# Projection phase of a hybrid mLSTM and attention layer: separate PSUM banks for units and operand products, and another order in the last block

## Chip, cores, metric

One core of a Trainium2 chip. The metric is the device time of one execution in microseconds (us); lower is better. The kernel runs one decoder layer over 2048 tokens of width 1024.

## What is computed

The layer is a sandwich-normalised token mixer and an MLP. The mixer has one combined input projection; its columns feed a 4-head mLSTM (a chunked linear recurrence with a causal convolution on q and k, a state C, and output gates) and an 8-head latent attention, whose q, k and v come by a second product from normalised low-rank latents. Cut to what matters:

```python
def token_mixer(a, cos, sin, w_in, ..., w_out):
    proj = a @ w_in
...
    qk_ml = jax.nn.silu(causal_conv(qk_ml, conv_w, conv_b))
...
    h_ml = mlstm_chunkwise(q_ml, k_ml, v_ml, gates[..., :ML_HEADS], gates[..., ML_HEADS:])
    h_ml = rmsnorm(h_ml, ml_head_norm)
    h_ml = h_ml * jax.nn.sigmoid(o_ml)
    q = rmsnorm(c_q, q_norm) @ w_uq            # rotary on 32 of 96 columns a head
    kv = rmsnorm(c_kv, kv_norm) @ w_ukv        # 64 of k and 64 of v a head
...
    h_mla = causal_block_attention(q, k, v)
    return jnp.concatenate([h_ml, h_mla], axis=-1) @ w_out
```

Then `x + rmsnorm(mix)`, and `x + rmsnorm(relu(m @ w_up) ** 2 @ w_down)`.

## The kernel before

Every fp32 product is three matmuls on values split into a high and a low part (mm3, L244 to L247): high by high, low by high, high by low. A "step" below is one such group of three.

The program is written by a small list scheduler, the class Plan (L125). Each operation names its engine, a planned duration, a key (smaller is more urgent), the operations it comes after, the rings it takes a buffer from and the operations that give a buffer back. Plan runs this once on the host and so fixes one static order for each engine; on the chip each engine goes through its own list in order, and waits where a semaphore is not there yet. An operation that waits therefore holds all that stands behind it on its engine.

**Projection.** The tokens go in four blocks of 512 (NB). In a block PE works on units of eight steps each: 13, 14, 15 the latents, 0 the gates and rotary keys of the recurrence, 1 to 4 the convolved q and k, 5 to 8 the values (here called mv_0 to mv_3, one for 128 tokens each), 9 to 12 the output gates (mm_9 to mm_12). From the latents come operand products: kp_0 to kp_3 and vp_0 to vp_3 of one step each, qp_0 to qp_3 and rp_0, rp_1 (the rotary part of q) of two steps each. MIXED and LASTLINE (L98, L323) list gates and products in the wished order, and from the list each gets its time, which is its key. In blocks 0 to 2 the values come ahead of MIXED; in block 3 LASTLINE has them last.

**PSUM.** Units and products share one ring, "mm", of two banks (psm, L306 and L310). A unit is read by one instruction: DVE for a gate (L1177), ACT for values (L1150). A k, v or q product is read by two: ACT copies the high part (L766, for v L817), DVE copies the raw value (L769, for v L820); both come after the product and are planned at 570 and 690 ns, and the ring's buffer is free when both are done. Pool then makes the low part (L772), and SP stores it (L796, L831, L844). An r product has three DVE readers (L876, L880, L883).

**Chunks.** chunk (L1181) does the recurrence for 128 tokens: scores S, a transpose kt, the numerator num (four matmuls on vext and the state C), the state products kv_c_0 and kv_c_1 (they need kw, which DVE makes from kt, L1243), then on DVE, ACT and Pool the normalised state hn (L1282), its transpose ht on PE (L1289), and ho = ht times the gate (L1293). hn has two buffers (HN), so hn of chunk 2 can only be written once ht of chunk 0 has been read.

**Into attention.** When the last unit is done, switch2 (L1436) gives the projection's space to attention. The row maxima of head 0 and query block 0 (m_0_0_0 and so on, L1578, reduced on DVE, L1583 and L1585; their transposes mt) come ahead of the scores S (L245 with QK). The QK operands are loaded on SP's queue: rotary keys krd (L1526), qkd (L1532), qrd (L1534), the mask (L1471).

## Time and profile before

| | |
|---|---|
| median of 3 runs | 2426.09 us (2425.77 to 2426.1) |
| profiled execution, span | 2425.1 us |
| mean granted clock of TensorE | 0.994 |
| busy: PE, DVE, ACT, POOL | 2375.4, 1750.1, 1363.0, 833.1 us |
| projection with the way into attention | about 0 to 550 us |

A row of the timeline shows start, duration, engine, line, operation, output<-inputs, and in brackets the idle time before it with what ended it. A row of the table by stretches shows for each engine busy time and number of instructions, then the clock granted to TensorE (PEclk, 1.00 is full), the DMA engines' share and GB/s. A matmul's row runs to the modelled end of its pipeline, so rows that follow each other overlap.

### The profile page before, as it was taken

The numbers are of one execution on the slowest core, as the hardware profiler recorded it, in microseconds if no ns is written. First come the engines' busy times: TensorE is split into PE (matmuls) and PEld (weight loads), VectorE is DVE, ScalarE is ACT, GpSimd is POOL, SyncE is SP. The second block draws the span as 40 slices with busy tenths as digits, with TensorE's granted clock in tenths as the row PEclk, the third lists the DMA queues.
The fourth block names the chain that finished last, engine by engine and source line by source line (L and its number), as shares of the span: only waits on it lengthen the run. The fifth ranks groups of instructions, "written<-read, shape, count | busy, mean of one in ns | idle before, by whom it ended". The sixth has DMA issues, their size and how long they took to land.

```text
span 2425.1 us, 33998 instructions
## 1 busy us (share of the span) xinstructions
PE 2375.4 (98%) x10943; PEld 1918.9 (79%) x10943; DVE 1750.1 (72%) x3149; ACT 1363.0 (56%) x2646; POOL 833.1 (34%) x717
## 2 busy tenths in 40 slices
PE   9899999999999999999999999999999999999996
PEld 7777787777777777788788888888888888888885
DVE  6966565658888887746866687766675677676778
ACT  5635454437778778544666566755664343443454
POOL 2635334437888888522000000000000322322346
PEclk9999999999999999999999999999999999999999
DMA  7686979789222321567877697666674545445458
GB/s 280 204 315 219 346 241 327 260 217 200 60 54 56 81 59 22 155 187 240 270 225 215 205 311 235 204 170 178 178 216 142 161 126 182 129 137 173 127 136 166
DMA packets 341307, 449.20 MB, mean 185 GB/s; under 512 B 34908, under 2 KB 227432, under 8 KB 341128
## 3 DMA queue, kind: packets, MB, share of 16 engines
q1 hardware_dynamic: 337192, 440.16, 59.4%
q0 software_dynamic: 3936, 6.87, 2.0%
q8 instruction: 86, 1.41, 0.2%
q14 instruction: 93, 0.76, 0.1%
HBM read 295.97 MB, written 153.05 MB: 185 GB/s over the span
## 4 chain that ended last, share of the span: by engine, by line
PE 54%; DVE 1%; DMA 0%; issue 0%; ACT 0%; DVEq 0%; POOL 0%; POOLq 0%; ACTq 0%
PE op L245 1%; PE op L247 1%; PE op L246 1%; PE d_0X L2519 1%; PE d_4X L2519 1%; PE d_0X L2520 1%; PE d_4X L2521 1%; PE d_2X L2519 1%; PE d_1X L2519 1%; PE d_1X L2520 1%; PE d_2X L2521 1%; PE d_3X L2519 1%; PE d_3X L2521 1%; PE d_1X L2521 1%; PE d_4X L2520 1%; PE d_3X L2520 1%
## 5 line engine op out<-in xcount | busy, mean ns | idle before, releaser
L2557 POOL TENSOR_TENSOR y<-vd_0X,y 128x512 f32<-128x512 f32 x7 | 10.6, 1514 | 725.4 <-ACT vd_0X L2554 725.4
L1642 ACT ACTIVATE ph<-S 128x512 fp32r<-128x512 f32 (+1 forms) x320 | 170.4, 533 | 87.2 <-PE S L247 53.3
L1677 POOL TENSOR_TENSOR t<-t,ph 128x512 f32<-128x512 f32 (+1 forms) x192 | 212.9, 1109 | 18.1 <-ACT ph L1642 7.7
L2469 ACT CAST hh<-hr 128x512 fp32r<-128x512 f32 (+1 forms) x208 | 116.4, 567 | 158.0 <-DMA hr<-hd 20.5
L1650 DVE TENSOR_TENSOR pl<-S,ph 128x512 fp32r<-128x512 f32 (+3 forms) x272 | 157.2, 589 | 30.5 <-ACT S L1646 27.7
L245 PE MATMUL mm<-xh,wh 128*128 128x512 f32 x384 | 159.1, 414 | 5.4 <-DVE ks L769 2.1
L2474 DVE TENSOR_TENSOR hl<-hr,hh 128x512 fp32r<-128x512 f32 (+1 forms) x208 | 133.3, 648 | 32.5 <-ACT hh L2469 26.3
L246 PE MATMUL mm<-xl,wh 128*128 128x512 f32 x384 | 150.9, 393 | 0.7 <-DVE xl L420 0.6
L247 PE MATMUL mm<-xh,wl 128*128 128x512 f32 x384 | 150.6, 392 | 0.5 <-DVE wl L495 0.5
L1583 DVE TENSOR_REDUCE mp<-m 128x1 f32<-128x512 f32 x192 | 128.6, 681 | 18.9 <-PE m L1578 18.1
L1646 ACT ACTIVATE S<-S 128x512 f32<-128x512 f32 (+3 forms) x272 | 140.8, 518 | 0.4
L245 PE MATMUL S<-QK 97*128 97x512 f32 (+1 forms) x320 | 120.8, 377 | 2.0 <-DVE pl L1650 1.9
L1663 PE MATMUL o<-ph,V 128*128 128x512 f32 (+1 forms) x320 | 118.8, 378 | 2.5 <-DVE ot L1736 2.1
L246 PE MATMUL S<-QK 97*128 97x512 f32 (+1 forms) x320 | 117.8, 368 | 0.0
L247 PE MATMUL S<-QK 97*128 97x512 f32 (+1 forms) x320 | 117.5, 367 | 0.0
L1578 PE MATMUL m<-QK 96*128 96x512 f32 (+3 forms) x320 | 116.5, 395 | 0.7 <-DVE mp L1585 0.5
L1666 PE MATMUL o<-pl,V 128*65 128x512 f32 (+1 forms) x320 | 115.6, 362 | 0.5 <-POOL pl L1650 0.5
L245 PE MATMUL op<-wo,hh 128*128 128x512 f32 x256 | 101.2, 395 | 1.7 <-DVE osm L1967 0.9
L247 PE MATMUL op<-wo,hl 128*128 128x512 f32 x256 | 99.9, 390 | 0.0
L246 PE MATMUL op<-wo,hh 128*128 128x512 f32 x256 | 99.8, 390 | 0.0
L2308 ACT ACTIVATE t<-t 128x512 f32<-128x512 f32 x96 | 60.6, 632 | 69.5 <-DVE t L2303 68.9
L245 PEld LDWEIGHTS mm<-xh,wh 128*128 128x128 f32 x384 | 72.4, 189 | 26.2 <-DVE ks L769 2.9
(6449 smaller groups left out, 7567.0 us busy)
## 6 DMA issues: line engine op xcount, KB each, us to landing
hr<-hd SPq DMA_DIRECT2D x100, 448.0 KB
wr<-in_wu_dram SPq DMA_DIRECT2D x71, 512.0 KB
hd<-t SPq DMA_DIRECT2D x128, 256.0 KB
hd<-ts SPq DMA_DIRECT2D x96, 256.0 KB
wl<-wparts SPq DMA_DIRECT2D x45, 512.0 KB
QK<-qkd SPq DMA_DIRECT2D x32, 512.0 KB
xt<-in_x_dram SPq DMA_DIRECT2D x28, 512.0 KB
xf<-xd SPq DMA_DIRECT2D x40, 256.0 KB
```

Of the source, the lines that this page charges most:

```text
L245: pe.matmul(o, ah, bh, start=start, stop=False)
L246: pe.matmul(o, ah, bl, start=False, stop=False)
L247: pe.matmul(o, al, bh, start=False, stop=stop)
L1578: pe.matmul(ps[:, :n], Qh[s][0:96, q0 : q0 + P], Kh[s][0:96, kb * TB : kb * TB + n], start=True, stop=True)
L1583: vec.tensor_reduce(mp["t"][:, j, kb : kb + 1], ps, axis=AX.X, op=ALU.max)
L1642: act.activation(t["h"][:, :w], t["S"][:, :w], AF.Exp)
L1646: act.activation(t["p"][:, :w], t["S"][:, :w], AF.Exp)
L1650: (pool if by_pool else vec).tensor_tensor(t["l"][:, :w], t["p"][:, :w], f32(t["h"][:, :w]), ALU.subtract)
L1663: pe.matmul(o0, v[:, 0:128], t["h"][:, :w], start=start, stop=stop)
L1677: pool.tensor_tensor(to, to, hv, ALU.add)
L2474: vec.tensor_tensor(t["l", m][:, :w], t["r", m][:, :w], f32(t["h", m][:, :w]), ALU.subtract)
L2519: pe.matmul(ps, a, w[:, 0], start=start, stop=False, skip_group_check=True)
```

## The change

1. **Banks.** The ring "mm" of two becomes "mma" and "mmb" of one each. Gate units (and in block 3 the value units, together the "fillers"), and of the other units the odd ones, are in mma; all operand products and the other units are in mmb. Unit 12 of block 3 is in mmb.
2. **Keys.** A filler's steps after the first get a key later by FILL = 14, and fillers of a block are chained by gate_end. So products come between a gate's steps, not behind it.
3. **Orders.** MIXED has unit 9 ahead of the k products. LASTLINE has the values first, with q and r products between them, then 16 (the weights of k and v), gates 9 to 12 with k and v products.
4. **Space in block 3.** The weights of 12, 17 and 18 go to buffers of qbd and kT, the staged v products to the ring of raw weights, and hn and ho share their buffers chunk by chunk.
5. **Into attention.** EARLY names (0, 0): the maxima of head 0, query block 0 take a bank and a key of their own ahead of the others. The mask's load has a later key, switch2 waits for the stores of v of block 3, and the load of V for query block 1 for the last chunk's ho.

In blocks 0 to 2 PE's order becomes products between gate steps: for block 0 (a count is of matmuls) before `kp_2 x3, kp_3 x3, kt_2, ptx, kv_2_0, vp_0 x3, mm_10 x12`, after `mm_10 x6, kt_2, mm_10 x6, kv_2_0, ptx, mm_10 x3, kp_3 x3`; and before `qp_0 x6, qp_1 x6, mm_12 x24, qp_2 x6, qp_3 x6, rp_0 x6, rp_1 x3`, after `qp_0 x6, mm_12 x6, qp_1 x6, mm_12 x6, qp_2 x6, mm_12 x6, qp_3 x6, mm_12 x6, rp_0 x6`. The line numbers of the changed kernel differ: L246 to L248 are its mm3, L1330 its ht.

PE in block 1, around the transposes of the normalised state (ht_1, ht_2), before:

```order
L1289 MATMUL ht_0_2662<-cst,hn_0_2257 128x128 x4
L1289 MATMUL ht_1_2669<-cst,hn_1_2364 128x128 x4
L245 MATMUL rp_1_2655<-ch_1996,wh_18_2506 128x512
L246 MATMUL rp_1_2655<-cl_1997,wh_18_2506 128x512
L247 MATMUL rp_1_2655<-ch_1996,wl_18_2530 128x512
L1289 MATMUL ht_2_2693<-cst,hn_2_2687 128x128 x4
L1232 MATMUL num_3_2698<-vext,E_3_2297 128x129 x2
```

and after (mm_13 is the first latent unit of block 2):

```order
L1330 MATMUL ht_1_2695<-cst,hn_1_2380 128x128 x4
L246 MATMUL mm_13_2676<-xh_2_2616,wh_13_2575 128x512
L247 MATMUL mm_13_2676<-xl_2_2626,wh_13_2575 128x512
L248 MATMUL mm_13_2676<-xh_2_2616,wl_13_2573 128x512
L246 MATMUL mm_13_2676<-xh_3_2624,wh_13_2575 128x512
L247 MATMUL mm_13_2676<-xl_3_2635,wh_13_2575 128x512
L248 MATMUL mm_13_2676<-xh_3_2624,wl_13_2573 128x512
L246 MATMUL mm_13_2676<-xh_4_2641,wh_13_2575 128x512
L247 MATMUL mm_13_2676<-xl_4_2670,wh_13_2575 128x512
L248 MATMUL mm_13_2676<-xh_4_2641,wl_13_2573 128x512
L1330 MATMUL ht_2_2722<-cst,hn_2_2714 128x128 x4
```

The rotary product's last step has left the place between ht_1 and ht_2, and nine matmuls of the next block's first unit stand there. In block 0 there are twelve: three of mm_13, six of rp_1, three of mm_13.

PE in block 3, at the k products, before (mm_9 is a gate, ch and cl the latent's two parts):

```order
L247 MATMUL mm_9_4356<-xh_7_3858,wl_9_4242 128x512
L245 MATMUL kp_1_4426<-ch_4369,wh_16_4182 128x512
L246 MATMUL kp_1_4426<-cl_4370,wh_16_4182 128x512
L247 MATMUL kp_1_4426<-ch_4369,wl_16_4180 128x512
L245 MATMUL kp_2_4430<-ch_4369,wh_16_4182 128x512
L246 MATMUL kp_2_4430<-cl_4370,wh_16_4182 128x512
L247 MATMUL kp_2_4430<-ch_4369,wl_16_4180 128x512
L245 MATMUL kp_3_4446<-ch_4369,wh_16_4182 128x512
```

and after (kv_2_1 and kt_3 belong to the recurrence's chunks 2 and 3):

```order
L248 MATMUL kp_0_4760<-ch_4375,wl_16_4689 128x512
L246 MATMUL mm_9_4774<-xh_0_3582,wh_9_4717 128x512
L247 MATMUL mm_9_4774<-xl_0_3625,wh_9_4717 128x512
L248 MATMUL mm_9_4774<-xh_0_3582,wl_9_4710 128x512
L1291 MATMUL kv_2_1_4784<-vext,kw_2_4715 128x258
L246 MATMUL mm_9_4774<-xh_1_3601,wh_9_4717 128x512
L247 MATMUL mm_9_4774<-xl_1_3653,wh_9_4717 128x512
L248 MATMUL mm_9_4774<-xh_1_3601,wl_9_4710 128x512
L246 MATMUL kp_1_4792<-ch_4375,wh_16_4702 128x512
L247 MATMUL kp_1_4792<-cl_4376,wh_16_4702 128x512
L248 MATMUL kp_1_4792<-ch_4375,wl_16_4689 128x512
L1280 MATMUL kt_3_4800<-cst,kT_117 128x128 x2
```

The k products stood in a row behind a gate unit that was done; now three or six matmuls of gate 9 stand between two of them. The whole of block 3 on PE, before: `mm_9 x15, kp_0, mm_9 x9, kp_1, kp_2, kp_3, vp_0, mm_10 x24, vp_1, vp_2, vp_3, mm_11 x24, qp_0, qp_1, mm_12 x24, qp_2, qp_3, rp_0, rp_1`, then the four value units with the chunks between them, m_0_0_0 right behind the last value unit and kt_3. After: `mv_0 x24, qp_0, mv_1 x6, qp_1, mv_1 x6, qp_2, mv_1 x12, qp_3, mv_2 x9, rp_0`, the chunks' work with rp_1 and the rest of the values, `num_2, kp_0, mm_9 x3, kv_2_1, mm_9 x3, kp_1, kt_3, mm_9 x6, kp_2, kv_3_0, mm_9 x3, num_3, kp_3, mm_9 x3, kv_3_1, mm_9 x6, vp_0, mm_10 x6, vp_1, mm_10 x18, vp_2, mm_11 x6, vp_3, mm_11 x18, mm_12 x15, m_0_0_0, mm_12 x6, m_0_1_0, mm_12 x3, m_0_2_0, m_0_3_0, ht_0, ht_1, mt_0`.

SP's queue at the first loads of QK, before (L1205 and L1197 belong to the chunks):

```order
L844 DMA qkd<-qs_3_4677 64x2x512
L901 DMA qrd<-rs_3_4700 256x1x512
L901 DMA qrd<-rs_3_4715 256x1x512
L1197 DMA E_2_4833<-wd_4301 128x512
L1471 DMA maskneg<-in_consts_dram 128x512
L1526 DMA QK_4792<-krd 32x2x512 x4
L1532 DMA QK_4792<-qkd 64x4x512
L1205 DMA iwbc_2_4839<-wd_4301 64x2x128 x2
L1534 DMA QK_4792<-qrd 16x2x512 x2
```

and after (L863 stores v of block 3, L1571, L1577 and L1579 load QK):

```order
L863 DMA vd<-vs_3_4886 128x1024
L863 DMA vd<-vs_3_4910 128x1024
L863 DMA vd<-vs_3_4936 128x1024
L1571 DMA QK_4964<-krd 32x2x512
L1577 DMA QK_4964<-qkd 64x4x512
L1579 DMA QK_4964<-qrd 16x2x512 x2
L1516 DMA maskneg<-in_consts_dram 128x512
L1571 DMA QK_4964<-krd 32x2x512 x3
L863 DMA vd<-vs_3_4970 128x1024
L1577 DMA QK_4964<-qkd 64x4x512
```

The loads stood behind the rotary stores and ahead of chunk 2; now they stand behind the stores of three v products, and one more store stands among them.

The diff, cut to its core:

```diff
-EARLY = ()
+EARLY = ((0, 0),)
...
-LASTLINE = [16, "k0", "k1", 9, "k2", "k3", "v0", 10, "v1", "v2", "v3", 11, 17, "q0", "q1", 12, "q2", "q3", 18, "r0", "r1", 5, 6, 7, 8]
+LASTLINE = [5, 17, "q0", "q1", 6, "q2", "q3", 18, 7, "r0", "r1", 8, 16, 9, "k0", "k1", 10, "k2", "k3", 11, "v0", "v1", 12, "v2", "v3"]
+FILL = 14.0
...
-    psm = pp(s_x, "psm", 2, "right")
+    psm = pp(s_x, "psm", 1, "right")
...
-    MIXED = [16, "k0", "k1", 9, "k2", "k3", "v0", 10, "v1", "v2", "v3", 11, 17, "q0", "q1", 12, "q2", "q3", 18, "r0", "r1"]
+    MIXED = [16, 9, "k0", "k1", "k2", "k3", "v0", 10, "v1", "v2", "v3", 11, 17, "q0", "q1", 12, "q2", "q3", 18, "r0", "r1"]
...
+        aside = b == NB - 1 and u in (12, 17, 18)
...
+        def aside_of(i):
+            if "a" not in t:
+                t["a"] = b1.tile([P, 2, n], F32R, tag=f"kT{(b + 1) % 2}" if u == 18 else f"qbd{(b + 1) % 2}", name=f"wa{b}_{u}")
+            return t["a"][:, i]
...
-        at = TIME[b][u]
+        at = TIME[b][5] if b == NB - 1 and 5 <= u <= 8 else TIME[b][u]
...
+        gl = pl.op("X", 0, place_l, [g, *o_turn], kA(b, at - LLEAD), take=() if aside else ("wl",))
...
+        if aside:
+            o_aside[u] = (c, gl)
...
+    def filler(b, u):
+        return u in GATES or b == NB - 1 and 5 <= u <= 8
+    def place_of(b, u):
+        return "mma" if filler(b, u) and (b, u) != (NB - 1, 12) or u in (13, 15, 1, 3, 5, 7) else "mmb"
...
+        t = {"at": place_of(b, u)}
+        fill = filler(b, u)
+        behind = [gate_end[b]] if b in gate_end and fill else []
...
+                "PE", PIN, lambda k=k: mm(k), [w["op"][k], *o_x[b, k]] + ([last] if k else behind), kA(b, TIME[b][u] + (FILL if k and fill else 0.0)),
+                take=() if k else (t["at"],), free=w["free"] + x_holders[b, k],
...
+        if fill:
+            gate_end[b] = last
...
-                    q["p"] = psm.tile([P, TB], F32, tag="mm", name=f"{nm}{b}_{n}")
+                    q["p"] = psm.tile([P, TB], F32, tag="mmb", name=f"{nm}{b}_{n}")
...
-            h = pl.op("Activation", 570, hi, [g, last], key - EV, free=[("mm", first)])
+            h = pl.op("Activation", 570, hi, [g, last], key - EV, free=[("mmb", first)])
...
-            d = pl.op("DVE", 690, raw, [g, last], key - EV, free=[("mm", first)])
+            d = pl.op("DVE", 690, raw, [g, last], key - EV, free=[("mmb", first)])
...
+                ring = "awr" if b == NB - 1 else "sg"
...
+                if ring == "awr":
+                    pl.group = "in"
...
+            fill = filler(b, 5 + c)
+            behind = [gate_end[b]] if b in gate_end and fill else []
...
+                    "PE", PIN, lambda k=k: mm(k), [ws[k // 2]["op"][0], *o_x[b, k]] + ([last] if k else behind), kA(b, TIME[b][5 + c] + (FILL if k and fill else 0.0)),
+                    take=() if k else (place_of(b, 5 + c),), free=ws[k // 2]["free"] + x_holders[b, k],
...
+        hn_, ho_ = ("hn", "ho") if b < NB - 1 else ("hn", "hn") if c < 2 else ("ho", "ho")
...
-    o_s2 = pl.op("Z", 0, switch2, unit_ops + [o_s1], -KEYA)
+    o_s2 = pl.op("Z", 0, switch2, unit_ops + [o_s1, *(o_vd[4 * NB - 4 + n] for n in range(4))], -KEYA)
...
-    o_mask = pl.op("SP", 500, lambda: dma(maskneg, consts[:, K_MASK : K_MASK + 512]), [o_s1], key=EKEY - 30, kb=256)
+    o_mask = pl.op("SP", 500, lambda: dma(maskneg, consts[:, K_MASK : K_MASK + 512]), [o_s1], key=EKEY - 29, kb=256)
...
-            after = [o_s2, o_const["v0"], *([o_sc[start_of[0, qb - 2]]] if qb > 1 else o_last if qb else [])]
+            after = [o_s2, o_const["v0"], *([o_sc[start_of[0, qb - 2]]] if qb > 1 else o_chunk[NB - 1, 3]["gate"] if qb else [])]
```

More of the change, by code (lines that the diff above doesn't have):

```diff
@@ L674, in one @@
             if b == 0:
-                o = pl.op("Activation", 560, evac, [u["op"], *t.get("o", [])], key, take=take, free=[("mm", u["head"])])
+                o = pl.op("Activation", 560, evac, [u["op"], *t.get("o", [])], key, take=take, free=[(u["at"], u["head"])])
                 head = o
@@ L678, in one @@
             else:
-                o = pl.op("DVE", 660, evac, [u["op"], o_rsbc[b], *t.get("o", [])], key, take=take, free=[("mm", u["head"]), ("rsbc", o_rsbc[b])])
+                o = pl.op("DVE", 660, evac, [u["op"], o_rsbc[b], *t.get("o", [])], key, take=take, free=[(u["at"], u["head"]), ("rsbc", o_rsbc[b])])
                 head = o
@@ L1062, in g13 @@
             vec.tensor_copy(t["tm"], t["p"][:, 0:48].rearrange("p (a c h) -> p a c h", a=3, c=4))
-        G = pl.op("DVE", 660, evac, [u["op"], o_rsbc[b]], key, take=("G",), free=[("mm", u["head"]), ("rsbc", o_rsbc[b])])
+        G = pl.op("DVE", 660, evac, [u["op"], o_rsbc[b]], key, take=("G",), free=[(u["at"], u["head"]), ("rsbc", o_rsbc[b])])
         rotate(b, t, G)
@@ L1320, in chunk @@
         o = pl.op("Pool", 1000, norm4, [o, o_fill], key)
-        hn = pl.op("DVE", 800, norm5, [o], key, take=("hn",), free=[("num", n)])
+        hn = pl.op("DVE", 800, norm5, [o], key, take=(hn_,), free=[("num", n)])
         gs = [o_gate[b, i] for i in range(4)]
-        h = pl.op("PE", 440, turn_h, [hn, *gs], key, take=("aS",), free=[("hn", hn)])
-        g = pl.op("DVE", 660, gated, [h], key, take=("ho",), free=[("aS", h)])
+        h = pl.op("PE", 440, turn_h, [hn, *gs], key, take=("aS",), free=[(hn_, hn)])
+        g = pl.op("DVE", 660, gated, [h], key, take=(ho_,), free=[("aS", h)])
         out["gate"] = [g]
-        out["end"] = pl.op("SP", 500, store, [g], key, free=[("ho", g)], kb=256)
+        out["end"] = pl.op("SP", 500, store, [g], key, free=[(ho_, g)], kb=256)
     def rope_tables():
@@ L1411, in trunk @@
             chunk(b, c)
+        if b == NB - 2:
+            for u in (17, 18):
+                for o in o_aside[u]:
+                    pl.ops[o][3].extend(x for c in range(4) for x in o_chunk[b, c]["qk"])
     V = {}
```

72 lines of the change are left out of this document (39 added, 33 removed).

## The prediction

> **What bounds the kernel now.** I read the page's head first, then the busy time of each engine by stretches of 25 us, then PE's waits up to 660 us, then the timeline at the waits that looked removable. The profiled execution has a span of 2425.1 us; the median of the runs is 2426.09, so about 1.0 us lies outside the span, and I carry that over unchanged.
>
> ```profile
> span 2425.1 us, 33998 instructions
> PE 2375.4 (98%) x10943; PEld 1918.9 (79%) x10943; DVE 1750.1 (72%) x3149; ACT 1363.0 (56%) x2646; POOL 833.1 (34%) x717
> ```
>
> PE is the bound, and the most that any re-ordering can win is what PE does not fill, plus what it runs at a lower clock. The stretches say where that is.
>
> ```profile
> core 0: us, PE busy (x) PEld busy (x) DVE busy (x) ACT busy (x) POOL busy (x), PEclk, DMA share, GB/s
> 75.00:100.00 25.00, 21.95 (x106) 17.76 (x105) 24.45 (x38) 16.23 (x30) 18.13 (x15) 1.00 0.51 150
> 100.00:125.00 25.00, 21.98 (x99) 16.89 (x98) 20.66 (x39) 15.16 (x36) 20.44 (x17) 1.00 0.85 283
> 125.00:150.00 25.00, 23.71 (x111) 18.45 (x110) 22.39 (x38) 14.16 (x26) 13.04 (x9) 1.00 0.87 300
> 225.00:250.00 25.00, 23.44 (x111) 18.35 (x110) 17.03 (x38) 14.41 (x41) 16.85 (x16) 1.00 0.90 305
> 350.00:375.00 25.00, 23.78 (x111) 18.33 (x110) 17.01 (x39) 14.63 (x42) 16.38 (x17) 1.00 0.92 312
> 450.00:475.00 25.00, 21.34 (x82) 15.37 (x81) 19.24 (x23) 13.72 (x26) 18.34 (x14) 0.93 0.80 260
> 525.00:550.00 25.00, 21.73 (x89) 16.17 (x88) 18.60 (x54) 7.78 (x23) 4.80 (x9) 0.73 1.07 237
> ```
>
> The holes are the products and gates of blocks 0 to 3 (75 to 150, 225 to 250, 350 to 375, 450 to 475) and the ramp into attention (525 to 550). In the last two the granted clock falls too: 0.07 of 25 us is 1.75 us lost in the first, 0.27 of 25 is 6.75 us in the second.
>
> ```profile
> PE ht L1289 <- DVE hn L1282: 2.9, 3, 1.2
> PE mt L1609 <- DVE mp L1583: 1.9, 1, 1.9
> PE kv L1250 <- DVE kw L1243: 1.0, 1, 1.0
> ```
>
> Those three rows (us in total, times, longest) are waits that the new order touches; the rest are waits for a PSUM bank, small and many.
>
> **How long a bank is away.** Block 3 shows it, start, duration, and in brackets the idle time before:
>
> ```profile
> 453.57 0.39 PE L246 MATMUL mm<-xl,wh 128*128 128x512 f32 x1
> 453.80 0.39 PE L247 MATMUL mm<-xh,wl 128*128 128x512 f32 x1
> 454.97 0.50 PE L245 MATMUL kp<-ch,wh 128*128 128x512 f32 x1 [0.78 <-DVE gate L1177]
> 455.31 0.39 PE L246 MATMUL kp<-cl,wh 128*128 128x512 f32 x1
> ...
> 458.41 0.50 PE L245 MATMUL kp<-ch,wh 128*128 128x512 f32 x1 [1.77 <-DVE ks L769]
> ...
> 458.98 0.40 PE L247 MATMUL kp<-ch,wl 128*128 128x512 f32 x1
> 459.48 0.69 DVE L769 COPY ks<-kp 128x512 f32<-128x512 f32 x1 [0.53 <-PE kp L247]
> 460.20 0.58 ACT L766 CAST ks<-kp 128x512 fp32r<-128x512 f32 x1 [2.63 <-DVE ks L769]
> 460.84 0.79 PE L245 MATMUL mm<-xh,wh 128*128 128x512 f32 x1 [0.32 <-ACT ks L766]
> ...
> 468.44 0.50 PE L245 MATMUL vp<-wh,ch 128*128 128x512 f32 x1 [0.23 <-DVE gate L1177]
> ...
> 469.66 0.50 PE L245 MATMUL vp<-wh,ch 128*128 128x512 f32 x1 [0.26 <-DVE vs L820]
> ...
> 470.92 0.50 PE L245 MATMUL mm<-xh,wh 128*128 128x512 f32 x1 [0.29 <-DVE vs L820]
> ```
>
> Matmuls start 0.23 us apart (453.57, 453.80), so a step of three takes 0.69. A gate's bank has one reader: from the start of its last matmul to the next use 1.17 us (453.80 to 454.97). An operand product's bank has two, and ACT begins only when DVE is done: 458.98 to 460.84 is 1.86 us. The scheduler's costs let the two run side by side (both wait for the product alone) and so leave two steps of fill, 7 x 0.23 = 1.61, where 1.86 is needed: 0.25 short at each such place. The first matmul after a wait takes 0.34 to the next instead of 0.23, so each wait costs 0.11 more; and a row lasts 0.39 while the next could start after 0.23, so each listed wait hides 0.16. I add 0.27 to a listed wait.
>
> The Trainium skill, "PSUM — Partial Sum Buffer", section "PSUM bank collisions raise a hardware error", says that two engines may not touch one bank's partitions at the same time, ACT against DVE included; the trace agrees, DVE's read and then ACT's, 1.86 us. By the scheduler's costs (reads side by side) the fill would cover it; by the rows it does not.
>
> **Block 3** is re-ordered: values first, q and r products inside them, gates with k and v products last. Removed are the six waits above: 0.78 + 1.77 + 0.32 + 0.23 + 0.26 + 0.29 = 3.65, plus 6 x 0.27 = 1.62, plus the 1.75 us of low clock there: 7.0. New places, by the two bank times against the matmuls that the new order puts between: qp_1 and qp_2 (six matmuls between) 0.26 each, kp_1 and kp_2 (six and a state instruction) 0.13, gates 10 and 11 behind one product (1.17 - 4 x 0.23) 0.25 each, each with 0.11: 1.94. And a product is now early against its input:
>
> ```profile
> 448.04 0.69 DVE L1097 TENSOR_TENSOR raw<-mm,rsbc 128x512 f32<-128x512 f32 x1 [0.43 <-PE mm L247]
> ...
> 452.24 2.95 POOL L725 TENSOR_TENSOR cl<-cca,ch 128x512 fp32r<-128x512 f32 x2
> ```
>
> The q products need both of these latents. They follow one value unit, 24 matmuls or 5.5 us behind the unit that DVE reads at 448.04, so at about 453.3; the second step wants the second latent, done at 455.2 if Pool keeps its place. I take 1.0 us, bounds 0 (Pool's order moves up) and 1.2. For ACT, which casts four more weights in that stretch, 0.35 as an estimate, between 0 and one cast of the kind above, 0.58. Block 3: 7.0 - 1.94 - 1.0 - 0.35 = **3.7 us gained**, bounds 2.5 to 5.
>
> **Blocks 0 to 2: normalised state and kw.**
>
> ```profile
> 138.35 1.03 PE L1289 MATMUL ht<-cst,hn 128*128 128x128 f32 x8
> 140.73 0.75 DVE L1282 TENSOR_TENSOR hn<-num,sm 128x256 f32<-128x256 f32 x2
> 141.29 0.68 PE L1289 MATMUL ht<-cst,hn 128*128 128x128 f32 x4 [1.20 <-DVE hn L1282]
> ...
> 269.90 0.68 PE L1289 MATMUL ht<-cst,hn 128*128 128x128 f32 x4 [1.11 <-DVE hn L1282]
> ...
> 527.33 0.77 PE L1289 MATMUL ht<-cst,hn 128*128 128x128 f32 x4 [0.55 <-DVE hn L1282]
> ...
> 103.88 0.42 DVE L1243 SCALAR_TENSOR_TENSOR kw<-kt,tm 128x256 f32<-128x256 f32 x1
> 104.36 0.70 PE L1250 MATMUL kv<-vext,kw 128*128 128x258 f32 x2 [1.01 <-DVE kw L1243]
> ```
>
> ht_2 waits for hn_2, which has a buffer only when ht_0 is done. Before, three matmuls (0.69 us) stand between; now twelve in block 0 (2.76) and nine in block 1 (2.07), and block 2, which has nine in the old order, has no wait on hn (the three of the waits view are these three rows, in blocks 0, 1 and 3). 1.20 + 1.11, and 0.17 hidden in each, make **2.65 us gained**; bounds 0 (the fill hides it only if DVE is not behind) and 2.65. In block 0 kv_2_0 came straight behind kt_2 and ptx; now six gate matmuls (1.38) stand between, and the wait of 1.01, 1.1 with its restart, is gone: **1.1 gained**, bounds 0.4 to 1.2.
>
> **Blocks 0 to 2: the bank waits themselves.** Going through both orders with 1.17 and 1.86, and 0.11 for each wait, I get 3.9, 3.95 and 3.3 us before and 3.5, 4.3 and 3.45 after: pairs of products no longer stand side by side, but every product now waits for the only operand bank, and q products with six gate matmuls between are 0.25 short (four a block). **0.1 lost.** These sums leave out that DVE may be late. With two banks in turn such lateness was half covered, with one it is not: the twelve q and r places of these blocks have no spare time. An instruction of 0.69 that is met half-way costs 0.35, and DVE is busy 0.68 (17.03 of 25) to 0.83 (20.66 of 25) of these stretches: about 0.25 each, 3.0 in all, of which I take half, since the order plans for some: **1.5 lost**, bounds 0 and the rival below.
>
> **The ramp.** The last gate units now end PE's projection work, and the first four maxima (h 0, q block 0) stand inside unit 12 instead of in the last chunk.
>
> ```profile
> 526.12 0.66 PE L1578 MATMUL m<-QK 96*128 96x128 f32 x3
> 539.35 0.63 PE L245 MATMUL S<-QK 97*128 97x512 f32 x1
> 548.09 0.43 PE L245 MATMUL S<-QK 97*128 97x512 f32 x1
> 504.38 2.59 SPq L1526 DMA_DIRECT2D QK<-krd x4
> ...
> DMA to landing us min/median/max: 2.1/4.2/4.6
> ```
>
> From the first maximum to the second head's scores 22 us pass, with DVE busy 18.6 of 25: it reduces the maxima, and it still must. What chunk 3 asked of DVE there is earlier now, but the last gate's chain and the bunched ho steps come in. The gain lies between 0 and 8.6 (the wait of mt, 1.85, and the 6.75 of clock); I take the value nearest to mt's wait, **1.5 gained**. Against it: the loads of QK stood on SP at 504.38, 21.7 us ahead of the first maximum. Now they stand behind the store of vs_2, whose product is 43 matmuls (9.9 us) ahead of that maximum. Evacuation 1.86, Pool's subtraction about 1.5, the store and four loads about 2.9 (0.65 each, from 2.59 for four) and 2.1 to 4.2 to land make 8.4 to 10.5, so the margin is +1.5 to -0.6. **0.3 lost**; behind a waiting maximum stand the rest of unit 12 and everything else on PE.
>
> **Sum:** -3.7 - 2.65 - 1.1 + 0.1 + 1.5 - 1.5 + 0.3 = -7.05. 2426.1 - 7.05 = 2419.05, so **2419 us**. Its own range, from the bounds, is 2414 to 2424. After the ramp nothing in the order of attention is changed that I price.
>
> **Rivals.**
> 1. *The only operand bank makes DVE's lateness visible everywhere (slower).* Place: the 56 products of the four blocks. Price: 0.69 / 2 x 0.83 = 0.29 each, 16.2 us; with the 1.5 taken out of the sum that is -8.55 + 16.2 = +7.65, 2433.7. It beats the gains from 0.15 us a product on. For it: 24.45 of 25 DVE at 75 to 100, and the 1.77 at 458.41, a product that waited for a DVE queue. Against it: the order is planned with DVE's queue in it. Chance 0.17.
> 2. *The loads of QK come late.* If SP or the stores are 5 us behind, PE stands at the first maximum and the gain shrinks to -7.05 + 5 = about -2, 2424. For it the margin above; against it the DMA engines' share of 0.80 at 450 to 475, which leaves room. Chance 0.15.
> 3. *The clock falls in the product stretches.* Short idle times now come at every product. Row: at 100 to 125 PE is idle 3 us and the clock stays 1.00; at 450 to 475 with a 1.77 us wait it falls, at a price of 1.75. One such fall in each of blocks 0 to 2 costs 5.25: -1.8, 2424.3. The Trainium skill, "TensorE: Matmul & The Clock Gate", section "A second HAM failure mode: psum-queue depth-cycling", speaks against this change: cycling through banks makes PE idle for moments between groups, and the clock goes down and up. The trace bears that out only in block 3. Chance 0.08.
> 4. *The ramp gives all of its 8.6:* -14.15, 2412. Chance 0.10.
>
> **How the numbers follow.** The forecast has 0.50. About 0.2%, 4.85 us, is what a measurement of this kernel can tell from no change. Faster by more: 0.44 of the forecast and 0.10 of rival 4, 0.54. Within: 0.06 of the forecast, 0.12 of rival 2, 0.06 of rival 3, 0.24. Slower: rival 1 with 0.17, and 0.05 of rivals 2 and 3 where their price is doubled, 0.22. Range: from rival 4's 2412 to 2429, which is rival 1 at 0.21 us a product; beyond lie half of rival 1 and the ends of the others.
>
> **What would show it.** Right: no wait of ht on hn in blocks 0 and 1, none of kv on kw above 0.3, no clock below 1.00 between 440 and 500, and waits at q products near 0.1 listed (0.26 less the hidden 0.16). Wrong: listed waits above 0.3 at most products (rival 1), a wait of m on a DMA (rival 2), PEclk under 1.00 in the three earlier stretches (rival 3), an S of the second head over 10 us earlier than 548 (rival 4). If attention itself, after 600, changes by more than 1 us, I have missed something that is not in this list.

## The result, and the profile after

| | before | changed |
|---|---|---|
| median of 10 runs each | 2425.84 us (2422.55 to 2429.15) | 2432.43 us (2430.65 to 2435.64) |
| ratio, 95% interval | | 1.0029 (1.002 to 1.0038) |
| profiled execution, span | 2425.1 us | 2432.3 us |

The change makes the kernel slower by about 6.6 us; forecast were 2419 us, 7 us faster, with 2412 to 2429 as the range. Single runs of one kernel differ by several us, so small terms below are read in the profiles, and differences between kernels by their ratio to the kernel before, run beside them on the same chip.

From the head of the page of the changed kernel:

```profile
PE 2380.7 (98%) x10943; PEld 1917.2 (79%) x10943; DVE 1752.5 (72%) x3149; ACT 1362.2 (56%) x2646; POOL 828.7 (34%) x717
```

The work is the same. Where PE waits and where its clock falls has moved. By stretches of 25 us, the changed kernel:

```profile
core 0: us, PE busy (x) PEld busy (x) DVE busy (x) ACT busy (x) POOL busy (x), PEclk, DMA share, GB/s
75.00:100.00 25.00, 23.53 (x111) 18.57 (x110) 24.31 (x36) 15.38 (x30) 18.63 (x16) 1.00 0.46 131
100.00:125.00 25.00, 23.78 (x105) 17.51 (x103) 21.43 (x43) 16.72 (x39) 21.97 (x19) 1.00 0.87 283
125.00:150.00 25.00, 24.05 (x109) 18.18 (x108) 21.21 (x34) 13.25 (x25) 11.01 (x8) 1.00 0.95 338
225.00:250.00 25.00, 22.27 (x106) 17.62 (x106) 18.89 (x40) 16.59 (x44) 18.41 (x17) 1.00 0.88 313
350.00:375.00 25.00, 24.16 (x117) 19.33 (x116) 17.01 (x42) 15.13 (x40) 17.61 (x18) 1.00 0.91 310
450.00:475.00 25.00, 23.83 (x101) 17.96 (x100) 18.96 (x21) 11.77 (x23) 14.81 (x12) 1.00 0.68 216
525.00:550.00 25.00, 19.72 (x79) 13.00 (x78) 16.87 (x45) 5.30 (x13) 3.18 (x8) 0.80 1.07 262
550.00:575.00 25.00, 20.06 (x106) 15.55 (x104) 16.62 (x35) 14.27 (x30) 14.26 (x13) 0.96 0.97 208
```

Block 0 (75 to 150) and block 3 (450 to 475) are fuller, and the clock of block 3 is whole. Block 1 (225 to 250) is emptier. The last row is where the loss lies: PE is idle for 4.94 us in a stretch of attention that the prediction did not price. PE's waits in the changed kernel up to 660 us (total, times, longest) give it a name:

```profile
PE o L1708 <- DVE ot L1781: 5.1, 2, 4.8
PE mm L246 <- DVE gate L1217: 2.7, 3, 1.4
PE mv L247 <- DMA wl<-wparts: 2.2, 2, 1.3
PE m L1623 <- DVE mp L1630: 2.1, 2, 1.1
PE m L1623 <- DMA QK<-qrd: 1.7, 1, 1.7
...
PE qp L247 <- POOL cl L749: 0.8, 1, 0.8
```

Two of these waits in the kernel before, for the same buffers:

```profile
PE o L1663 <- DVE ot L1736: 0.9, 2, 0.6
...
PE m L1578 <- DVE mp L1585: 0.5, 1, 0.5
```

The first line is the largest of the changed kernel, and was 0.9 before. "ot" is the buffer in which an attention output is put together for its store to hT; there is one. So I followed what held it. Here is the changed kernel's timeline around that wait, ACT, DVE and PE:

```profile
573.40 0.58 ACT L1778 COPY ot<-o 64x512 f32<-64x512 f32 x1 [5.16 <-DMA hT<-ot]
574.02 0.68 DVE L1781 TENSOR_TENSOR ot<-ot,o 64x512 f32<-64x512 f32 x1 [5.05 <-ACT ot L1778]
574.84 0.76 PE L1708 MATMUL o<-ph,V 128*128 128x512 f32 x1 [4.85 <-DVE ot L1781]
...
575.90 0.63 PE L1708 MATMUL o<-ph,V 128*128 128x512 f32 x1
...
580.40 0.40 PE L1708 MATMUL o<-ph,V 128*128 128x512 f32 x1
```

Read from the bottom of the chain: PE's bank o is released by DVE, DVE waits for ACT's copy, ACT for the store of the output before it. After the wait PE's matmuls take 0.63 to 0.76 us until about 579.5, and 0.40 then: a second price, in clock. The Trainium skill, "TensorE: Matmul & The Clock Gate", section "What's actually happening", says that PE falls to half rate after an idle window of about 3.4 us and needs as long a busy one to rise; the trace agrees here, with 4.85 us of idle time and some 4.7 us of slow matmuls. It does not agree at 458.41 of the kernel before, in the prediction's rows, where the matmuls are slow after a wait of 1.77 us with 0.78 us some microseconds ahead of it.

That store stands on SP's queue. SP in the changed kernel, from the first load of QK on:

```profile
519.13 0.63 SPq L1571 DMA_DIRECT2D QK<-krd  x1
...
531.13 2.75 SPq L1579 DMA_DIRECT2D QK<-qrd  x2
533.98 3.16 SPq L1592 DMA_DIRECT2D V<-vd  x4
537.24 5.00 SPq L1338 DMA_DIRECT2D hT<-ho  x4
542.29 2.86 SPq L1592 DMA_DIRECT2D V<-vd  x4
...
566.60 0.54 SPq L1791 DMA_DIRECT2D hT<-ot  x1
```

The same queue in the kernel before:

```profile
524.79 8.84 SPq L1547 DMA_DIRECT2D V<-vd  x8
533.73 4.28 SPq L1297 DMA_DIRECT2D hT<-ho  x2
...
557.65 0.49 SPq L1746 DMA_DIRECT2D hT<-ot  x1
```

QK's loads begin 14.8 us later (504.38 before, in the prediction's rows), V's 9.2 us later, and the first output's store 8.95 us later. The eight loads of V stood together; now four, then the four stores of ho, then four. The last unit, whose space V takes, also ends later: its last matmul starts at 530.62, against 524.90 before.

What is late at the first output is its place on SP. Pool's last instruction on it ends at 559.53 in the changed kernel, and its store is issued at 566.60, 7.1 us later; before, the two stand at 557.63 and 557.65. Below I call this gap the store's wait on SP.

In numbers, from the first matmul of unit 0 to the next such mark in the two profiles: start-up +1.2 us (unit 0 begins between 26.1 and 27.5 us in the profiles of fifteen kernels here, with no order by edit, so I take this for scatter), blocks 0 to 2 +1.3, block 3 to the first score S of head 0 +0.2, from there to the first score of head 1 +5.7 (60.8 before, 66.5 after), the rest -1.3; together, within rounding, the 7.2 us between the spans.

### The profile page after: what moved, and what is told of

Its sections match the earlier page's. It is cut to its first block, busy times and chain, and to the rows that moved or that the text cites. A ratio compares the mean times of both kernels' runs of the same rounds, so it can differ in the third digit from the quotient of the medians.

```text
span 2432.3 us, 33983 instructions
## 1 busy us (share of the span) xinstructions
PE 2380.7 (98%) x10943; PEld 1917.2 (79%) x10943; DVE 1752.5 (72%) x3149; ACT 1362.2 (56%) x2646; POOL 828.7 (34%) x717
## 4 chain that ended last, share of the span: by engine, by line
PE 53%; DVE 1%; issue 0%; DMA 0%; ACT 0%; POOL 0%; DVEq 0%; SPq 0%; POOLq 0%; ACTq 0%
PE op L246 1%; PE op L248 1%; PE op L247 1%; PE d_4X L2564 1%; PE d_3X L2566 1%; PE d_2X L2566 1%; PE d_1X L2566 1%; PE d_4X L2565 1%; PE d_4X L2566 1%; PE d_3X L2565 1%; PE d_2X L2565 1%; PE d_1X L2565 1%; PE d_1X L2564 1%; PE d_3X L2564 1%; PE d_2X L2564 1%; PE d_6X L2564 1%
## 5 line engine op out<-in xcount | busy, mean ns | idle before, releaser
L246 PE MATMUL mm<-xh,wh 128*128 128x512 f32 x376 | 155.5, 414 | 4.0 <-DVE gate L1217 2.7
L248 PE MATMUL mm<-xh,wl 128*128 128x512 f32 x376 | 147.5, 392 | 1.1 <-DVE wl L506 1.1
L246 PE MATMUL S<-QK 97*128 97x512 f32 (+1 forms) x320 | 120.7, 377 | 2.2 <-DVE pl L1695 1.9
L248 PE MATMUL S<-QK 97*128 97x512 f32 (+1 forms) x320 | 116.9, 365 | 0.0
L246 PE MATMUL op<-wo,hh 128*128 128x512 f32 x256 | 101.0, 394 | 1.2 <-DVE osm L2012 0.7
L248 PE MATMUL op<-wo,hl 128*128 128x512 f32 x256 | 99.8, 390 | 0.0
L246 PEld LDWEIGHTS mm<-xh,wh 128*128 128x128 f32 x376 | 70.6, 188 | 22.6 <-DVE gate L1217 5.3
```

What stands on the lines that cost most here:

```text
L246: pe.matmul(o, ah, bh, start=start, stop=False)
L248: pe.matmul(o, al, bh, start=False, stop=stop)
```

## Theories and experiments

**R, the ramp:** the way into attention (early maxima, QK's loads behind the v products) costs the time. **B, the banks:** one operand bank costs it, all through the four blocks. After the first four runs R was narrowed to what stands on SP's queue: V's loads, the new condition on them, the first output's store. The expectations call its forms S (the space that QK and V take), V (V's loads as a whole) and C (the condition on V alone). A difference in us is that of the medians on the same chip, 5 to 11 runs of each changed kernel; the ratio is the comparison's own, which parts from the quotient of the medians by up to 0.0005, 1.2 us (in before_v_late).

Each edit goes through the scheduler, which lays the lists of PE and DVE anew from some place on: with ot_first from the maxima of head 0, query block 3 on, with the condition on V from head 0's first score on. A run therefore shows what an edit is worth with the order that follows from it; the place on SP's queue alone and PE's new order were not run apart.

**Undo the early maxima.** Label no_early.

```diff
-EARLY = ((0, 0),)
+EARLY = ()
```

> The changed kernel with the first maxima back behind unit 12 (no early maxima), all else changed. Theory R (the loss is made at the end of block 3 and in the ramp: the first maximum waits 1.71 us for its QK load inside unit 12, so unit 12 ends 3 us late, so V is loaded late, so the first output store is late and PE waits 4.85 us for the accumulator): unit 12 ends near 527.6 instead of 530.6, the wait of m on the QK load is gone, the 4.85 shrinks to about 2, and the time falls by 3 to 5 us to 2427.5 to 2429.5. Rival B (the only operand bank costs it in the four blocks): within 1 us of the changed kernel, 2432.

Measured: 2432.98 us, +5.3, ratio 1.0025 (1.0014 to 1.0035), no different from the changed kernel; R's number is missed. The maxima themselves are not the cause: the wait of m for QK's loads is only larger (3.8 us), and the wait for ot smaller (2.3 us at its longest):

```profile
PE m L1623 <- DMA QK<-qrd: 3.8, 1, 3.8
```

**Block 3 in the old order, the banks still split.** Label old_last; the buffers of block 3, the early maxima and the condition on V are put back as well.

```diff
...
-LASTLINE = [5, 17, "q0", "q1", 6, "q2", "q3", 18, 7, "r0", "r1", 8, 16, 9, "k0", "k1", 10, "k2", "k3", 11, "v0", "v1", 12, "v2", "v3"]
+LASTLINE = [16, "k0", "k1", 9, "k2", "k3", "v0", 10, "v1", "v2", "v3", 11, 17, "q0", "q1", 12, "q2", "q3", 18, "r0", "r1", 5, 6, 7, 8]
...
-        return u in GATES or b == NB - 1 and 5 <= u <= 8
+        return u in GATES
...
```

> The changed kernel with block 3 in the old order (values last, old chunk buffers, no early maxima), but with the split banks, the later keys of gate steps and the new order of blocks 0 to 2. Theory R: the ramp is that of the kernel before, only blocks 0 to 2 with their plus of 1.3 us are left: 2426 to 2428. Rival B: all four blocks still run on one operand bank, so nearly the whole 6.6 us stays: 2430 or more.

Measured: 2431.99 us, +4.4, 1.0023 (1.0012 to 1.0033). So the old order does not bring the time back, and B has something. But the loss sits elsewhere: from unit 0 of block 3 to the last unit's last matmul this profile needs 110.5 us against 107.8 before. Products in a row on one bank cost 2.7 us in block 3; the split of the banks needs the new order there.

**QK's loads ahead.** Label qk_first: on SP the load of head 0, q block 0 comes ahead of the stores of the first three v products.

```diff
...
+                    if b == NB - 1 and n < 3:
+                        tc.add_manual_dep(
+                            nc.cur_bb.bb.instructions[-1], qk_load[-1].name, mybir.DependencyInfo(mybir.DependencyClass.NoSync, mybir.DependencyReason.DATA), reason="order"
+                        )
...
```

> The changed kernel with the load of QK of head 0, query block 0 put ahead of the stores of the first three v products on SP's queue. Theory R: the wait of 1.71 us at the first maximum is gone, unit 12 ends 1.7 us or more earlier, the later stores of v hurt little: 1 to 3 us less than the changed kernel, about 2430. Rival B: no difference beyond 0.5 us. A third way: the v stores are late instead and hold the loads of V, then it is slower.

Measured: 2435.13 us, +7.5, 1.0036 (1.0022 to 1.005). In the median nothing was won, though in the profile the first score of head 0 came 3.3 us earlier (538.8 against 542.1) and head 1 4.1 us earlier (604.5 against 608.6). The profiled run, 2432.05, is the fastest of only five, so the profile does not show what holds the median up. V's loads still began at 532.8, and the first output's store still waited 5.6 us on SP.

**The first output's store ahead.** Label ot_first: on SP it comes ahead of the QK loads of head 1, q blocks 2 and 3.

```diff
...
+            if h == 1 and b > 1:
+                tc.add_manual_dep(nc.cur_bb.bb.instructions[-1], out_first[-1].name, mybir.DependencyInfo(mybir.DependencyClass.NoSync, mybir.DependencyReason.DATA), reason="order")
...
```

> The changed kernel with the first output store of attention put ahead of the loads of QK for head 1, query blocks 2 and 3. Theory R: the copy that waits 5.16 us for that store's buffer goes, PE's wait of 4.85 us falls below 1, and the time falls by about 4 us to 2428.5. Rival: the wait was a cover for late loads, PE stands at the next S or o instead, and the time falls by less than 1 us.

Measured: 2430.41 us, +2.8, 1.0011 (1.0002 to 1.002): 3.8 us less than the changed kernel, with two intervals that just touch. The store's wait on SP is 0.03 us, and PE's wait for ot is gone. This turned me from PE's order to SP's. The same edit on the kernel before shows that the place isn't simply better:

> The kernel before with the first output store of attention ahead of the loads of QK for head 1, query blocks 2 and 3, and nothing else. Theory V: before, the first store does not wait on SP (it is issued 0.02 us after Pool's result), so nothing is gained: within 1.5 us of the kernel before. Rival (the order on SP is worth 3 us everywhere): 2423 or less.

Measured: 2426.02 us, -0.2, 0.9998 (0.9989 to 1.0006). Before, the store is not late, and moving it gains nothing.

**Make V late in the kernel before.** Label before_v_late: before, with the first V loads ordered on SP behind the last store of ho, and nothing of the change in it. An extra condition in before, and a manual order on SP that is not shown:

```diff
...
-            after = [o_s2, o_const["v0"], *([o_sc[start_of[0, qb - 2]]] if qb > 1 else o_last if qb else [])]
+            after = [o_chunk[NB - 1, 3]["end"], o_s2, o_const["v0"], *([o_sc[start_of[0, qb - 2]]] if qb > 1 else o_last if qb else [])]
...
```

> The kernel before, with nothing changed but the first loads of V put behind the last store of the recurrence's output on SP's queue, so that they start near 538 instead of 525, as late as in the changed kernel or later. Theory S: the loads behind them and the first output store slide by as much, a wait for the accumulator of 4 to 6 us comes, and the time is 4 to 8 us longer than before. Rival B: it has two banks in turn and no late loads that matter, so within 1 us of the kernel before.

Measured: 2433.56 us, +7.0, 1.0024 (1.0014 to 1.0033; 1.0024 is 5.8 us). Late V loads, with the order that follows from them, cost about what the whole change costs. SP in this run:

```profile
529.52 8.74 SPq L1299 DMA_DIRECT2D hT<-ho  x2
538.36 1.61 SPq L1550 DMA_DIRECT2D V<-vd  x3
...
565.59 0.49 SPq L1753 DMA_DIRECT2D hT<-ot  x1
```

V begins 13.6 us later than before and the first output's store 7.9 us later (9.2 and 8.95 in the changed kernel). Of the 7.9 us, 4.6 are the store's wait on SP; the output itself is done 3.3 us later.

**k and v products in the middle of block 3.** Label kv_mid: QK's operands are ready earlier, the gates 10 to 12 last.

```diff
-LASTLINE = [5, 17, "q0", "q1", 6, "q2", "q3", 18, 7, "r0", "r1", 8, 16, 9, "k0", "k1", 10, "k2", "k3", 11, "v0", "v1", 12, "v2", "v3"]
+LASTLINE = [5, 17, "q0", "q1", 6, "q2", "q3", 18, 7, "r0", "r1", 8, 16, "k0", "k1", "k2", "k3", "v0", "v1", 9, "v2", "v3", 10, 11, 12]
...
-        aside = b == NB - 1 and u in (12, 17, 18)
+        aside = b == NB - 1 and u in (16, 17, 18)
...
```

> The changed kernel with another order in block 3: the k and v products stand among the last value unit and gate 9, behind the q and r products, and gates 10 to 12 run without products; the weights of unit 16 take the side buffer in place of those of 12. Theory S (space): QK of head 0 takes the space in which the latents' parts lie that the last k and v products read, so its loads cannot start before the last v product, and the loads of V, of head 1 and the first output store, all on SP's queue, are 9 us late. With the last v product 8 us earlier the first load of QK is issued near 510 instead of 519, the wait of PE for the accumulator (4.85) is gone, and the time falls by 5 to 7 us to 2425.5 to 2427.5. Rival B (one operand bank): products still go through the one bank, 2431 to 2433.

Measured: 2432.95 us, +6.4, 1.0024 (1.0015 to 1.0032); theory S's number is missed. The loads of QK begin at 507.67 and m no longer waits for them; the first score of head 0 comes at 537.5. And the time is lost later, with V at 530.0 and a longer wait of PE for ot. SP's waits from 500 to 600 us, and the timeline of ACT and PE:

```profile
SPq L1592 <- PE mm L248: 7.2, 1, 7.2
```

```profile
569.44 0.58 ACT L1778 COPY ot<-o 64x512 f32<-64x512 f32 x1 [8.13 <-DMA hT<-ot]
...
570.88 0.77 PE L1708 MATMUL o<-ph,V 128*128 128x512 f32 x1 [7.83 <-DVE ot L1781]
```

SP stands for 7.2 us at V, whose space the last unit gives free (switch2), and PE, which now runs into attention early, waits for outputs that cannot be stored: the first is done at 552.89 and its store issued at 563.22.

**Tell the scheduler that the two readers come one behind the other.** Label serial: in the plan ACT's read of an operand bank comes after DVE's, as the trace has it.

```diff
-            h = pl.op("Activation", 570, hi, [g, last], key - EV, free=[("mmb", first)])
+            d = pl.op("DVE", 690, raw, [g, last], key - EV, free=[("mmb", first)])
             o_staged[b].append(g)
-            d = pl.op("DVE", 690, raw, [g, last], key - EV, free=[("mmb", first)])
+            h = pl.op("Activation", 570, hi, [g, last, d], key - EV, free=[("mmb", first)])
...
```

The v products get the same.

> The changed kernel with the scheduler told that ACT reads an operand bank only after DVE has read it, so that it leaves three steps of fill between products where it left two. Theory S: the block waits shrink by 1 to 3 us but the late loads stay, 2430 to 2432. Rival B: the waits of the one bank were the cost, and 4 us or more go, 2428 or less.

Measured: 2442.07 us, +15.6, 1.0061 (1.0049 to 1.0074). The more honest plan is the worst kernel of all, and its expectation missed. Block 0 takes 144.6 us instead of 134.2: the planner spreads products into the next block's units, where PE, in this run's timeline, meets the rotary products' readers:

```profile
151.22 0.50 PE L246 MATMUL rp<-ch,wh 128*128 128x512 f32 x1 [3.17 <-DVE rt L919]
```

Both edits together, label kv_mid_serial:

> Both: k and v products early in block 3, and the scheduler told of the two reads one after the other. Theory S: 2424 to 2426, up to 2 us less than with the early products alone. Rival B: what it falls by is what the scheduler's knowledge alone brings.

Measured: 2439.75 us, +13.2, 1.0049 (1.0037 to 1.0062): the same loss, and nothing that tells R and B apart.

**kv_mid without early maxima.** Label kv_mid_no_early, with EARLY = () on top of kv_mid.

> The changed kernel with the early k and v products in block 3 and without the early maxima. Theory V (in all profiles so far head 1's first scores start 70 to 76 us after the first load of V is issued, and that load waits for two things: the last projection unit, whose space V takes, and the loads of QK ahead of it on SP): here QK is loaded early and nothing stands inside the last units, so V starts at 525 to 527 as before, head 1 starts at 600 to 602, and the time is 2425 to 2428, about that of the kernel before. Rival (the space of the latents alone decides): the same as the kernel with early products and early maxima, 2431 to 2433.

Measured: 2431.64 us, +5.4, 1.0023 (1.0014 to 1.0032), no different from kv_mid; theory V's number is missed. V begins only 2.4 us later than before here, but SP's timeline shows its loads split by the stores of ho:

```profile
527.21 2.03 SPq L1592 DMA_DIRECT2D V<-vd  x4
531.20 3.27 SPq L1338 DMA_DIRECT2D hT<-ho  x4
534.52 2.70 SPq L1592 DMA_DIRECT2D V<-vd  x4
...
557.73 0.54 SPq L1791 DMA_DIRECT2D hT<-ot  x1
```

The store is issued about when it was before (557.65). But the output is done early here, and stands for 10.5 us until SP comes to its store:

```profile
545.96 1.29 POOL L1788 TENSOR_TENSOR ot<-ot,ou 64x512 f32<-64x512 f32 x1 [5.49 <-PE S L248]
```

The next output's copies wait, 5.51 us on ACT for this store and 5.14 on DVE for the store of the row sums behind it, and PE behind them, 4.46 us at a maximum and 2.65 at a score.

**And with the old condition on V.** Label kv_mid_no_early_v, the one line that differs:

```diff
-            after = [o_s2, o_const["v0"], *([o_sc[start_of[0, qb - 2]]] if qb > 1 else o_chunk[NB - 1, 3]["gate"] if qb else [])]
+            after = [o_s2, o_const["v0"], *([o_sc[start_of[0, qb - 2]]] if qb > 1 else o_last if qb else [])]
```

> Early k and v products, no early maxima, and that condition undone, but the first output store left behind the loads of QK. Between 2431.6 (without the undone condition) and 2424.6 (with the store moved too): if the condition is the larger part 2426 to 2428, if the store is, 2429 to 2431.

Measured: 2425.28 us, -0.8, 0.9997 (0.9988 to 1.0006). One condition is worth 6.2 us, and the two intervals don't meet. Its queue, and Pool at the first output:

```profile
527.71 6.02 SPq L1592 DMA_DIRECT2D V<-vd  x8
533.83 3.69 SPq L1338 DMA_DIRECT2D hT<-ho  x4
...
557.37 0.49 SPq L1791 DMA_DIRECT2D hT<-ot  x1
```

```profile
556.07 1.28 POOL L1788 TENSOR_TENSOR ot<-ot,ou 64x512 f32<-64x512 f32 x1
```

The eight loads stand together again, and the store follows Pool by 0.02 us. The first score of head 0 comes later, at 539.1 against 535.3, behind five more maxima on PE's list, so PE's order has a part in the 6.2 us that is not measured by itself. The new condition holds the second four of these eight loads until the last chunk's ho; with gate 12 as the last unit all four ho come at the very end, and their stores take SP first. This kernel has the one operand bank in all four blocks and is level with before, so B falls as the cause of the loss as a whole.

The same with ot_first's order too, label kv_mid_best:

> The same, with the loads of V for query block 1 free of the last chunk's gate product again (as before the change) and with the first output store of attention ahead of the loads of QK for head 1, query blocks 2 and 3. Theory V: V starts at 525 to 527, head 1 starts 3 to 5 us earlier against V's start, at 596 to 598, and the time is 2421 to 2425, less than both kernels. Rival: no more than 1 us less than the one without these two.

Measured: 2424.62 us, -1.6, 0.9996 (0.9987 to 1.0004): the lowest median that I found, some 8 us under the changed kernel, and not to be told from before.

**The condition alone, in the changed kernel.** Label v_cond is the changed kernel with the one line above; v_cond_ot has ot_first's order as well.

> The changed kernel with one condition undone: the loads of V for query block 1 wait for the recurrence's small loads of the last chunk, as before the change, and not for its gate product, so they stand ahead of the output stores of the recurrence on SP. If this condition is what makes the loads late (theory C): head 1 starts 3 to 5 us earlier than in the changed kernel and the time falls to 2427 to 2429. If the last unit and the QK loads decide (theory V): V still starts near 534, the time falls by less than 1.5 us, 2431 to 2433.

> The changed kernel with that condition undone and the first output store ahead of the loads of QK for head 1, query blocks 2 and 3, so that of the way into attention only the late last unit, the early maxima and the late QK loads are left. Theory V: 2429 to 2431, 2 to 3 us less than the changed kernel through the store. Theory C: 2425 to 2427.

Measured: v_cond 2429.77 us, +3.7, 1.0015 (1.0006 to 1.0024); v_cond_ot 2428.76 us, +2.7, 1.0013 (1.0004 to 1.0022). The condition is worth about 2.9 us here (the intervals still touch the changed kernel's), less than the 6.2 in kv_mid_no_early, and V still begins late, behind QK's loads: SP's first V load in v_cond comes at 531.12, 6.3 us behind before's 524.79. Both numbers lie between those of the theories. Part of the loss is the condition, part the place of the k and v products; undoing both, and the early maxima with them, ends it.

**All runs in one stretch.** From 540 to 620 us I add up PE's idle time and the time lost to the clock (20 us times what PEclk lacks), by four slices of 20 us. These are the first slices of two of the kernels, before:

```profile
540.00:560.00 20.00, 20.00 (x96) 15.83 (x96) 14.82 (x34) 12.57 (x28) 12.20 (x16) 0.80 1.10 228
```

and before_v_late:

```profile
540.00:560.00 20.00, 20.00 (x76) 15.51 (x75) 13.47 (x31) 9.42 (x22) 7.59 (x12) 0.60 1.11 244
```

PE is "busy" for the whole 20 us in both rows, and does 96 matmuls in one and 76 in the other: what is missing stands in the clock's column.

| kernel | first V load | store's wait on SP | idle | clock | idle + clock, to before | measured, to before |
|---|---|---|---|---|---|---|
| before | 524.8 | 0.0 | 0.9 | 4.0 | | |
| changed | 534.0 | 7.1 | 6.1 | 6.2 | +7.4 | +6.6 |
| no_early | 532.5 | 4.8 | 2.5 | 9.4 | +7.1 | +5.3 |
| kv_mid | 530.0 | 10.3 | 8.7 | 3.4 | +7.2 | +6.4 |
| kv_mid_no_early | 527.2, split | 10.5 | 8.7 | 3.4 | +7.2 | +5.4 |
| before_v_late | 538.4 | 4.6 | 1.7 | 9.6 | +6.4 | +7.0 |
| qk_first | 532.8 | 5.6 | 2.5 | 8.0 | +5.6 | +7.5 |
| ot_first | 534.7 | 0.0 | 1.0 | 8.6 | +4.7 | +2.8 |
| v_cond | 531.1 | 3.3 | 0.9 | 6.8 | +2.8 | +3.7 |
| v_cond_ot | 530.2 | 0.0 | 0.5 | 7.0 | +2.6 | +2.7 |
| old_last | 526.4 | 1.9 | 1.1 | 6.0 | +2.2 | +4.4 |
| before_ot_first | 522.4 | 0.0 | 1.7 | 4.4 | +1.2 | -0.2 |
| kv_mid_no_early_v | 527.7 | 0.0 | 0.8 | 3.8 | -0.2 | -0.8 |
| kv_mid_best | 526.6 | 0.0 | 0.6 | 4.0 | -0.3 | -1.6 |

This one stretch gives the measured difference within 2.2 us in every row, in kernels with different orders of block 3 (in old_last 2.7 us more lie ahead of it, in block 3). It sets one execution against medians; against the spans of the same executions it is off by up to 3.7 us (kv_mid_no_early, +3.5 in the span), since it leaves out what block 3 gained ahead of it. serial and kv_mid_serial, which lose their time in the blocks, are not in the table.

Where the store waits 3.3 us or more on SP, the kernel loses 3.7 to 7.5 us; where it does not wait, -1.6 to 2.8. The loss does not grow with the wait: 10.5 us of it cost 5.4, 4.6 cost 7.0. The 2.7 and 2.8 us that v_cond_ot and ot_first still lose come with a first output that is itself done 3 to 5 us later than before. Whether the loss shows as idle time or as clock differs from kernel to kernel.

## Why the prediction was wrong

**The step that failed** is the one that had no term: "After the ramp nothing in the order of attention is changed that I price." The lists there are changed. PE's is: where one maximum stood between head 0's first two scores, two maxima and four transposes mt stand now. And SP's is, by two edits that I had listed in the change and costed at nothing: k and v products at the end of block 3 move QK's loads (504.38 to 519.13), and these move V's; and the new condition on V lets the stores of ho in between. Head 1 then begins 5.7 us later, counted from head 0's first score. I had followed SP's queue up to the first maximum and priced 0.3 us there; I should have followed it to the next consumer, V, and to the first store behind that. My own test, a change of attention by more than 1 us, says so for the stretch before 600; the rest after head 1's first score is 1.3 us shorter.

In sum, the forecast misses the span's difference by 14.3 us: 5.7 of them lie in attention up to head 1, 5.1 in block 3 with the ramp, 3.5 in blocks 0 to 2; start-up and rest cancel.

**Block 3** was right: 3.7 us forecast. From 420 to 525 us before has 3.77 us idle and 1.75 lost to the clock; the changed kernel has 1.88 idle and no clock below 1.00: 3.6 gained. The wait of a q product for the second latent, taken at 1.0, is 0.8. These two rows are the last two slices of that stretch in the changed kernel:

```profile
475.00:500.00 25.00, 24.87 (x126) 20.61 (x124) 16.00 (x44) 14.71 (x42) 14.54 (x16) 1.00 0.67 219
500.00:525.00 25.00, 24.42 (x108) 19.19 (x107) 12.18 (x27) 7.17 (x18) 12.21 (x12) 1.00 0.66 185
```

**The ramp** was forecast at 1.2 gained (1.5, less 0.3 for QK). From block 3's start to the first score it took 122.4 us instead of 122.2, so it gave back the whole 3.6 of block 3, and some 0.2 more. Rival 2 happened in its mechanism, at a third of its price; the changed kernel's timeline of the first maximum and of unit 12's end:

```profile
527.59 0.30 PE L1623 MATMUL m<-QK 96*128 96x128 f32 x1 [1.71 <-DMA QK<-qrd]
...
530.62 0.63 PE L248 MATMUL mm<-xh,wa 128*128 128x512 f32 x1
```

1.71 us of unit 12, with the rest of the unit behind it. My margin of +1.5 to -0.6 us was too kind by 1.1. The 1.5 us, set nearest to mt's wait, were gained at mt and lost ahead of it: mt's wait of 1.9 is 0.2 now, and the maxima wait 2.1 us for DVE's reductions, where they waited 0.5. DVE still had to reduce them, as the prediction itself says. What share of that the bunched ho steps on DVE have, which I named and did not price, no run takes apart.

**Blocks 0 to 2** were forecast at 2.15 gained and cost 0.9 (mean of the eleven profiles with split banks against the three without, serial left out). By block: block 0 gains 1.9 (forecast 2.4), block 1 loses 1.9 (forecast 0.4 gained), block 2 loses 0.8 (forecast 0.65 lost). Waits of ht on hn are gone in blocks 0 and 1, as forecast, and kw's wait is gone in block 0. Block 1 failed, where the changed kernel's PE waits anew:

```profile
199.53 0.50 PE L247 MATMUL mv<-wl,xh 128*128 128x512 f32 x1 [1.32 <-DMA wl<-wparts]
...
234.89 0.70 PE L1291 MATMUL kv<-vext,kw 128*128 128x258 f32 x2 [0.57 <-DVE kw L1284]
236.81 0.50 PE L246 MATMUL mm<-xh,wh 128*128 128x512 f32 x1 [0.53 <-DVE gate L1217]
248.91 0.50 PE L246 MATMUL mm<-xh,wh 128*128 128x512 f32 x1 [1.36 <-DVE gate L1217]
```

The first row is a value unit that waits for the load of its low weights, and the sum has no term for it. Such waits come in block 1 of all eleven profiles with split banks and in block 2 of nine, together 0.7 to 3.2 us, in the mean 1.8 (1.2 in block 1, 0.6 in block 2), and in none of the three without; so they are most of what these two blocks lost. Why the load is not there in time was not followed: it is issued at 192.62, and at 192.96 before, where PE does not wait for it. Two gates wait for the gate bank, mma, not for the operand bank: a gate follows a gate there too closely. I had counted both kinds of bank with fixed times and put the lateness of DVE only on q and r products. For these the forecast held: the waits view lists one wait of a q product on the operand bank's readers and one of an r product, 0.3 us each.

**The rivals.** Rival 1 forecast 2433.7, next to what was measured, by a mechanism that was not there: waits at most products, against the few of the view above. That its number is near is chance; kv_mid_no_early_v, with its bank and without its loss, shows it. Rival 3 did not happen: the clock is 1.00 in all five stretches between 75 and 375 us, with 0.84 to 2.73 us of idle time in each 25. What the Trainium skill says in "TensorE: Matmul & The Clock Gate", section "A second HAM failure mode: psum-queue depth-cycling", the trace does not bear out for this kernel. Rival 4 did not happen, but its sign was misread: the score at 548.09 that the prediction takes for the second head's is the fifth of head 0, the first of its query block 1 (head 0 has 40). Before, the second head begins here:

```profile
600.13 0.40 PE L245 MATMUL S<-QK 97*128 97x512 f32 x1
```

So the 22 us from the first maximum lead to head 0's second query block, and the ramp to head 1 was 74 us long.

**What stays open:** whether kv_mid with early maxima and the old condition would be as good as kv_mid_no_early_v; how the loss divides between SP's queue and the order that the scheduler gave PE with each edit; why the low clock lasts longer in before_v_late, where no wait of PE above 0.5 us is listed between 535 and 575; and what sets the landing time of the first output's store, 6.2 to 7.1 us in the six profiles of the table where a copy waits for it (in before none waits).
